# Binary cross-entropy on one core: compute pieces of 8192 columns in place of 2048, and larger chunks at both ends

## The chip, the cores and the metric

The kernel runs on one NeuronCore of one Trainium2 chip. The metric is the device time of one execution in microseconds (us), as the median of several executions.

## The reference

Two 8192 x 8192 fp32 arrays come in, one goes out. The target holds only zeros and ones.

```python
def reference(pred, target):
    eps = 1e-7
    pred = np.clip(pred, eps, 1 - eps)
    return -(target * np.log(pred) + (1 - target) * np.log(1 - pred))
```

Since the target is 0 or 1, the kernel computes -ln|target - 1 + clip(pred)|. The target is cast to bf16 while it is loaded.

## The kernel before

The 524288 columns (per partition) are cut into chunks that are loaded and stored whole, in a ring of 32768 columns, a buffer whose places are used again in turn. Two chunks of 16384 fit in it; each half is called a slot below. A chunk is computed in pieces of `SUB` = 2048 columns.

```python
RING = 32768
SUB = 2048
LAG = 1

def chunk_widths(total):
    head = [4096, 4096, 8192]
    tail = [8192, 4096, 2048, 1024, 1024]
    big = 16384
    ...                                            # 30 chunks of 16384 between them

def front(c, w):
    p, t = ring_p[:, c : c + w], ring_t[:, c : c + w]
    nc.vector.tensor_scalar(out=p, in0=p, ...)     # L88, clamp
    nc.vector.scalar_tensor_tensor(out=p, in0=t, scalar=1.0, in1=p, ...)   # L91, t - 1 + p
    nc.scalar.activation(out=p, in_=p, func=Act.Abs)                       # L94
    nc.scalar.activation(out=p, in_=p, func=Act.Ln)                        # L95

def back(c, w):
    nc.vector.tensor_scalar(out=p, in0=p, scalar1=-1.0, ...)               # L99, negate
...
def finish_one():
    nonlocal stored
    k, c, w, last = waiting.pop(0)
    back(c, w)
    if last:
        store(k)                # on the GpSimd queue
        stored = k + 1
        load_what_fits()        # target (cast), then prediction, GpSimd queue

for k, c, w, last in pieces:
    front(c, w)
    waiting.append((k, c, w, last))
    if len(waiting) > LAG:
        finish_one()
    if last and cols[k] + widths[k] <= total - RING // 2:
        while waiting:          # a chunk is finished before the next one begins
            finish_one()
```

## Time and profile before

| | before |
|---|---|
| time | 1873.39 us, median of 3 (1873.09 to 1873.55) |
| span of the profiled execution | 1873.0 us |
| instructions | 1564 (VectorE 772, ScalarE 516) |
| VectorE / ScalarE busy | 63% / 52% |
| HBM traffic | 805 MB, 430 GB/s over the span |
| one big chunk, landing to landing | 58.22 us |

The last row comes from the timeline: the first clamp of the first big chunk starts at 81.60 us, that of the last at 1769.93, with 29 chunks between them.

In the lines of the profile DVE is VectorE, ACT is ScalarE, POOL is GpSimd and SP is SyncE; a transfer is issued by an engine and lands when its data has arrived. These are lines of the page of the kernel before: busy time per engine (share of the span, number of instructions), the DMA row of the 40 slices (9 is 90% or more), and the DMA queues (packets, MB, share of the 16 engines' span).

```profile
span 1873.0 us, 1564 instructions
...
DVE 1178.3 (63%) x772; ACT 976.3 (52%) x516; POOL 64.2 (3%) x117
...
DMA  9999999999999999999999999999999999999997
...
q14 instruction: 11, 0.09, 0.0%
HBM read 536.87 MB, written 268.44 MB: 430 GB/s over the span
...
```

The reader is to see that DMA is full in 39 slices of 40 while neither compute engine is. Queue q14, which the profile labels instruction, is read here as the fetching of the instructions themselves.

These are groups of the same kernel with different shapes kept apart: count, then busy us and the mean ns of one, then idle time before them.

```profile
...
L91 DVE SCALAR_TENSOR_TENSOR ring_p<-ring_t,ring_p 128x2048 f32<-128x2048 bf16 x255 | 584.6, 2292 | 9.9 <-DMA ring_t<-in_target_dram 1.2
...
L88 DVE TENSOR_SCALAR ring_p<-ring_p 128x2048 f32<-128x2048 f32 x255 | 311.6, 1222 | 552.3 <-DMA ring_p<-in_pred_dram 552.3
...
L91 DVE SCALAR_TENSOR_TENSOR ring_p<-ring_t,ring_p 128x1024 f32<-128x1024 bf16 x2 | 2.5, 1226 | 0.1
...
```

An operation on 2048 columns takes nearly twice as long as on 1024 (2292 against 1226 ns), so the fixed part is only 2 x 1226 - 2292 = 160 ns.

Now the timeline of the kernel before, near the end: start, duration, engine, line, operation; in brackets the idle time before it and what ended it.

```profile
...
1731.55 0.53 POOL L80 DMA_DIRECT2D ring_p<-in_pred_dram  x1 [35.86 <-DMA out_dram<-ring_p]
...
1752.57 0.54 POOL L84 DMA_DIRECT2D out_dram<-ring_p  x1 [20.49 <-DVE ring_p L99]
...
1769.93 1.23 DVE L88 TENSOR_SCALAR ring_p<-ring_p 128x2048 f32<-128x2048 f32 x1 [17.66 <-DMA ring_p<-in_pred_dram]
...
1789.51 0.53 POOL L80 DMA_DIRECT2D ring_p<-in_pred_dram  x1 [35.88 <-DMA out_dram<-ring_p]
...
1808.89 1.48 POOL L80 DMA_DIRECT2D ring_p<-in_pred_dram  x1 [9.17 <-DMA ring_p<-in_pred_dram]
1809.02 1.23 DVE L99 TENSOR_SCALAR ring_p<-ring_p 128x2048 f32<-128x2048 f32 x1 [2.78 <-ACT ring_p L95]
...
1850.94 0.53 POOL L84 DMA_DIRECT2D out_dram<-ring_p  x1 [1.77 <-DVE ring_p L99]
```

This is how the rotation is read. A prediction load issued at 1731.55 lets a clamp start at 1769.93. The store of the other slot is issued at 1752.57, while that load is under way, and lands at 1789.51, when the waiting prediction load goes out. Each transfer waits for those issued before it. Compute of the chunk takes from 1769.93 to the end of the last negate at 1809.02 + 1.23, 40.3 us. The issue at 1808.89 took 1.48 us instead of 0.54: it ended with the negate beside it.

Finally two rows of who waited for whom (us in total, times, longest), of the kernel before.

```profile
...
POOL ring_p L80 <- DMA out_dram<-ring_p: 1087.8, 30, 37.1
...
DVE ring_p L88 <- DMA ring_p<-in_pred_dram: 552.3, 32, 18.5
...
```

GpSimd waits for stores to land in 30 chunks, and VectorE's clamp for loads, about 18 us a chunk. VectorE has time to spare.

### The profile page before, as it was taken

The numbers are of one execution on the slowest core, as the hardware profiler recorded it, in microseconds if no ns is written. First come the engines' busy times: TensorE is split into PE (matmuls) and PEld (weight loads), VectorE is DVE, ScalarE is ACT, GpSimd is POOL, SyncE is SP. The second block draws the span as 40 slices with busy tenths as digits, with TensorE's granted clock in tenths as the row PEclk, the third lists the DMA queues.
The fourth block names the chain that finished last, engine by engine and source line by source line (L and its number), as shares of the span: only waits on it lengthen the run. The fifth ranks groups of instructions, "written<-read, shape, count | busy, mean of one in ns | idle before, by whom it ended". The sixth has DMA issues, their size and how long they took to land.

```text
span 1873.0 us, 1564 instructions
## 1 busy us (share of the span) xinstructions
DVE 1178.3 (63%) x772; ACT 976.3 (52%) x516; POOL 64.2 (3%) x117
## 2 busy tenths in 40 slices
DVE  4557755577555775557755567655676556765594
ACT  3446544465444664446644466444564445654474
POOL 1000000000000000000000000000000000000010
DMA  9999999999999999999999999999999999999997
GB/s 302 359 347 346 347 392 385 341 336 358 383 386 350 337 351 377 393 352 339 353 366 392 363 337 353 357 393 373 337 348 350 393 385 336 340 357 384 393 319 323
DMA packets 16427, 671.19 MB, mean 358 GB/s; under 512 B 1824, under 2 KB 1824, under 8 KB 2720
## 3 DMA queue, kind: packets, MB, share of 16 engines
q0 software_dynamic: 16272, 669.00, 99.4%
q1 hardware_dynamic: 144, 2.10, 0.3%
q14 instruction: 11, 0.09, 0.0%
HBM read 536.87 MB, written 268.44 MB: 430 GB/s over the span
## 4 chain that ended last, share of the span: by engine, by line
DMA 36%; issue 27%; DVE 27%; ACT 7%; POOL 1%; another core or an unknown queue 1%; POOLq 0%; PEldq 0%
DMA ring_p<-in_pred_dram 32%; DVE ring_p L91 13%; DVE ring_p L99 7%; DVE ring_p L88 7%; DMA out_dram<-ring_p 4%; ACT ring_p L94 3%; ACT ring_p L95 3%; POOL out_dram L84 1%; POOL ring_t L75 0%; POOL ring_p L80 0%; POOLq L175 0%; POOLq L84 0%; PEldq L175 0%
## 5 line engine op out<-in xcount | busy, mean ns | idle before, releaser
L94 ACT ACTIVATE ring_p<-ring_p 128x2048 f32<-128x2048 f32 (+1 forms) x257 | 488.9, 1902 | 864.8 <-DVE ring_p L91 864.8
L88 DVE TENSOR_SCALAR ring_p<-ring_p 128x2048 f32<-128x2048 f32 (+1 forms) x257 | 313.0, 1218 | 552.3 <-DMA ring_p<-in_pred_dram 552.3
L91 DVE SCALAR_TENSOR_TENSOR ring_p<-ring_t,ring_p 128x2048 f32<-128x2048 bf16 (+1 forms) x257 | 587.0, 2284 | 10.0 <-DMA ring_t<-in_target_dram 1.2
L95 ACT ACTIVATE ring_p<-ring_p 128x2048 f32<-128x2048 f32 (+1 forms) x257 | 489.2, 1903 | 8.1
L99 DVE TENSOR_SCALAR ring_p<-ring_p 128x2048 f32<-128x2048 f32 (+1 forms) x257 | 313.0, 1218 | 109.3 <-ACT ring_p L95 109.3
L80 POOL DMA_DIRECT2D ring_p<-in_pred_dram x37 | 21.3, 576 | 1097.0 <-DMA out_dram<-ring_p 1087.8
L84 POOL DMA_DIRECT2D out_dram<-ring_p x38 | 21.7, 571 | 684.8 <-DVE ring_p L99 681.1
L75 POOL DMA_DIRECT2D ring_t<-in_target_dram x38 | 21.5, 567 | 5.3 <-DMA ring_t<-in_target_dram 4.4
L127 ACT ACT_TABLE_LOAD x1 | 1.3, 1283 | 0.7 <-PEq L164 0.7
L126 DVE MEMSET warm<- 1x8 f32 x1 | 0.1, 65 | 0.8 <-PEq L164 0.8
L127 ACT ACTIVATE warm<-warm 1x8 f32<-1x8 f32 x1 | 0.2, 208 | 0.0
L164 POOL MEMSET const-float32-0.0<- 128x1 f32 x1 | 0.1, 99 | 0.2 <-issue 0.2
L164 POOL MEMSET const-bfloat16-1.0<- 128x1 bf16 x1 | 0.1, 102 | 0.0
L164 POOL MEMSET const-float32-1.0<- 128x1 f32 x1 | 0.1, 100 | 0.0
L164 POOL MEMSET const-uint8-127<- 128x1 uint8 x1 | 0.1, 99 | 0.0
## 6 DMA issues: line engine op xcount, KB each, us to landing
ring_t<-in_target_dram POOLq DMA_DIRECT2D x30, 4096.0 KB, 55.8
ring_p<-in_pred_dram POOLq DMA_DIRECT2D x2, 4096.0 KB, 29.0
out_dram<-ring_p POOLq DMA_DIRECT2D x2, 4096.0 KB, 30.6
out_dram<-ring_p POOLq DMA_DIRECT2D x3, 2048.0 KB, 54.1
ring_p<-in_pred_dram POOLq DMA_DIRECT2D x2, 2048.0 KB, 24.2
ring_t<-in_target_dram POOLq DMA_DIRECT2D x2, 2048.0 KB, 37.8
ring_t<-in_target_dram POOLq DMA_DIRECT2D x3, 1024.0 KB, 16.2
ring_p<-in_pred_dram SPq DMA_DIRECT2D x1, 2048.0 KB, 10.2
```

What stands on the lines that cost most here:

```text
L75: nc.gpsimd.dma_start(out=ring_t[:, c : c + w], in_=dram(target_f, cols[k], w))
L80: queue.dma_start(out=ring_p[:, c : c + w], in_=dram(pred_f, cols[k], w))
L84: nc.gpsimd.dma_start(out=dram(out_f, cols[k], w), in_=ring_p[:, c : c + w])
L88: nc.vector.tensor_scalar(out=p, in0=p, scalar1=EPS, scalar2=1 - EPS, op0=Alu.max, op1=Alu.min)
L91: nc.vector.scalar_tensor_tensor(out=p, in0=t, scalar=1.0, in1=p, op0=Alu.subtract, op1=Alu.add)
L94: nc.scalar.activation(out=p, in_=p, func=Act.Abs)
L95: nc.scalar.activation(out=p, in_=p, func=Act.Ln)
L99: nc.vector.tensor_scalar(out=p, in0=p, scalar1=-1.0, scalar2=None, op0=Alu.mult)
L126: nc.vector.memset(warm, 1.0)
L127: nc.scalar.activation(out=warm, in_=warm, func=Act.Ln)
L164: nc = _bacc.Bacc("TRN2", target_bir_lowering=False, num_devices=1)
```

## The change

The intent is to do the compute with a quarter of the instructions: a chunk of 16384 columns becomes two pieces of 8192. Head and tail are loaded in chunks of 8192, and the last two chunks are stored piece by piece, so that the end still drains in small steps.

```diff
-SUB = 2048
-LAG = 1
-def chunk_widths(total):
-    head = [4096, 4096, 8192]
-    tail = [8192, 4096, 2048, 1024, 1024]
-    big = 16384
+BIG = 16384
+def plan(total):
+    head = [(8192, [4096, 4096]), (8192, [8192])]
+    tail = [(8192, [4096, 4096]), (8192, [4096, 2048, 1024, 1024])]
+    n = (total - sum(w for w, _ in head + tail)) // BIG
+    chunks = head + [(BIG, [BIG // 2] * 2)] * n + tail
...
+    def store(k, off, w):
+        nc.gpsimd.dma_start(
+            out=dram(out_f, k)[:, off : off + w], in_=span(ring_p, cols[k] + off, w)
+        )
...
+    def finish_one():
+        nonlocal stored
+        k, off, w = waiting.pop(0)
+        back(cols[k] + off, w)
+        if k >= tail:
+            store(k, off, w)
+        elif off + w == widths[k]:
+            store(k, 0, widths[k])
+        else:
+            return
+        stored = cols[k] + off + w
+        load_what_fits()
```

The operations of `front` and `back`, the ring and the queues stay as they were. In the changed kernel the clamp is L85, the subtract-add L88, Abs and Ln L91 and L92, the negate L96, the store L79, the prediction load L76.

More of the change, by code (lines that the diff above doesn't have):

```diff
@@ L12 @@
 RING = 32768
-SUB = 2048
-LAG = 1
-def chunk_widths(total):
-    head = [4096, 4096, 8192]
-    tail = [8192, 4096, 2048, 1024, 1024]
-    big = 16384
-    n = (total - sum(head) - sum(tail)) // big
-    widths = head + [big] * n + tail
-    assert sum(widths) == total
-    return widths
+BIG = 16384
[4 more added lines that the diff above has]
+    chunks = head + [(BIG, [BIG // 2] * 2)] * n + tail
+    assert sum(w for w, _ in chunks) == total
+    return chunks, len(chunks) - len(tail)
 @with_exitstack
@@ L55 @@
     total = R * C // P
-    def dram(flat, col, w):
-        return flat[col * P : (col + w) * P].rearrange("(p w) -> p w", p=P)
     pool = ctx.enter_context(tc.tile_pool(name="rings", bufs=1))
@@ L63, with dram, span, load @@
     warm = pool.tile([1, 8], fp32, name="warm", tag="warm")
-    widths = chunk_widths(total)
-    cols = [sum(widths[:k]) for k in range(len(widths))]
-    def at(k):
-        c = cols[k] % RING
-        assert c + widths[k] <= RING
-        return c
-    def load_t(k):
-        c, w = at(k), widths[k]
-        nc.gpsimd.dma_start(out=ring_t[:, c : c + w], in_=dram(target_f, cols[k], w))
-    def load_p(k):
-        c, w = at(k), widths[k]
-        queue = nc.sync if k == 0 else nc.gpsimd
-        queue.dma_start(out=ring_p[:, c : c + w], in_=dram(pred_f, cols[k], w))
-    def store(k):
-        c, w = at(k), widths[k]
-        nc.gpsimd.dma_start(out=dram(out_f, cols[k], w), in_=ring_p[:, c : c + w])
-    def front(c, w):
-        p, t = ring_p[:, c : c + w], ring_t[:, c : c + w]
+    chunks, tail = plan(total)
+    widths = [w for w, _ in chunks]
+    cols = [sum(widths[:k]) for k in range(len(chunks))]
+    def dram(flat, k):
+        part = flat[cols[k] * P : (cols[k] + widths[k]) * P]
+        return part.rearrange("(p w) -> p w", p=P)
+    def span(ring, col, w):
+        c = col % RING
+        assert c + w <= RING
+        return ring[:, c : c + w]
+    def load(k):
+        queue = nc.sync if k == 0 else nc.gpsimd
+        nc.gpsimd.dma_start(out=span(ring_t, cols[k], widths[k]), in_=dram(target_f, k))
+        queue.dma_start(out=span(ring_p, cols[k], widths[k]), in_=dram(pred_f, k))
+    def store(k, off, w):
+        nc.gpsimd.dma_start(
+            out=dram(out_f, k)[:, off : off + w], in_=span(ring_p, cols[k] + off, w)
+        )
+    def front(col, w):
+        p, t = span(ring_p, col, w), span(ring_t, col, w)
         nc.vector.tensor_scalar(
@@ L95, in front, with back @@
         nc.scalar.activation(out=p, in_=p, func=Act.Ln)
-    def back(c, w):
-        p = ring_p[:, c : c + w]
-        nc.vector.tensor_scalar(
-            out=p, in0=p, scalar1=-1.0, scalar2=None, op0=Alu.mult
-        )
-    pieces = []
-    for k, w in enumerate(widths):
-        n = max(1, w // SUB)
-        for i in range(n):
-            pieces.append((k, at(k) + i * (w // n), w // n, i == n - 1))
-    stored = 0
-    loaded = 0
+    def back(col, w):
+        p = span(ring_p, col, w)
+        nc.vector.tensor_scalar(out=p, in0=p, scalar1=-1.0, scalar2=None, op0=Alu.mult)
+    stored = loaded = 0
     def load_what_fits():
@@ L116, in load_what_fits @@
         while (
-            loaded < len(widths)
-            and cols[loaded] + widths[loaded] <= (cols + [total])[stored] + RING
-        ):
-            load_t(loaded)
-            load_p(loaded)
+            loaded < len(chunks) and cols[loaded] + widths[loaded] <= stored + RING
+        ):
+            load(loaded)
             loaded += 1
+    waiting = []
+    def finish_one():
[10 more added lines that the diff above has]
+        load_what_fits()
     with tc.manual_schedule():
@@ L127 @@
         nc.scalar.activation(out=warm, in_=warm, func=Act.Ln)
-        waiting = []
-        def finish_one():
-            nonlocal stored
-            k, c, w, last = waiting.pop(0)
-            back(c, w)
-            if last:
-                store(k)
-                stored = k + 1
-                load_what_fits()
-        for k, c, w, last in pieces:
-            front(c, w)
-            waiting.append((k, c, w, last))
-            if len(waiting) > LAG:
+        for k, (_, pieces) in enumerate(chunks):
+            off = 0
+            for w in pieces:
+                front(cols[k] + off, w)
+                waiting.append((k, off, w))
+                off += w
+                if len(waiting) > 1:
+                    finish_one()
+            while waiting and k < tail:
                 finish_one()
-            if last and cols[k] + widths[k] <= total - RING // 2:
-                while waiting:
-                    finish_one()
         while waiting:
```

## The prediction

> **What bounds the kernel now.** The DMA engines. In the page's 40 slices DMA stands at 9 tenths in 39. The stretches view gives a DMA share of 1.00 in every 116.5 us period, and near 1.00 from 4 to 1860 us. HBM traffic is 430 GB/s over the span. The Trainium skill ("DMA: Bandwidth & Descriptors", Specifications) gives 435 GB/s as the fabric ceiling; this trace agrees: two 16384-column chunks (50.3 MB) take 116.5 us, 432 GB/s. VectorE is 63% busy, ScalarE 52%.
>
> Transfers behave like one first-in-first-out list, about 19.4 us for one chunk's target load, prediction load or store: a prediction load lands 38.4 us after issue (a target load is ahead of it), a store 37, a target load 55.8. The rotation is store k, target k+2, prediction k+2, store k+1. A bubble opens only if store k+1 is issued after prediction k+2 lands, so a chunk's compute may take about 58 us less the start of a transfer, some 56 us. In the timeline it takes 40.3 us (1769.9 to 1810.3).
>
> **What the change does.** 257 pieces become 69: VectorE 772 to about 208 instructions, ScalarE 516 to about 140. By the groups kept apart by shape, 1024/2048 columns take 0.69/1.22 us (clamp, negate), 1.23/2.29 (subtract-add), 1.05/1.91 (Abs, Ln): a fixed part of only 0.15 to 0.2 us. I estimate 4.4, 8.7 and 7.0 us at 8192 columns; VectorE sheds about 54 us of busy time, ScalarE about 75, none on the critical path.
>
> What grows is the fill of the pipeline in each chunk: two fronts 26 us, Ln of the second piece ends at 41, the last negate at 45.7. Compute per chunk goes from 40.3 to about 46 us; about 10 us of slack remain.
>
> Issue blocking: the Trainium skill ("SBUF — State Buffer", the "DVE blocks DMA" trap) says that GpSimd cannot write descriptors during a two-port VectorE instruction. The trace agrees: issues beside a clamp or negate took 0.96 to 1.48 us instead of 0.54, ending 0.1 us after it. At 8192 columns a block may last 4.4 us. In the steady state stores are issued with VectorE idle, and the prediction load falls into the second subtract-add with a target load still queued: no bubble.
>
> Head: the first 32768 columns are issued at once in both kernels and keep the DMA busy to 81.6 us; the first two stores come at about 47 and 80 us, in time. Tail: the loads end near 1828 us; the last big store is issued near 1818, the piece stores at 1832 to 1857, each before its turn. The list ends as before. The 4.4 and 9.2 us issue waits before the last small loads, which cost nothing, disappear. DMA operations fall from 114 to 106, bytes unchanged.
>
> **Prediction: 1873 us, range 1867 to 1880.** Faster by over 2%: 0.01; within 2%: 0.97; slower: 0.02.
>
> **What would show it.** DMA share 1.00 in periods of 116.5 us; VectorE near 1125 us busy, ScalarE near 901; the clamp's wait for the prediction load falls from about 18 to about 12 us per chunk; stores land about 31 us after issue instead of 37; the last store issued near 1857.
>
> **What would make it wrong.** Compute above 56 us per chunk (large pieces slower than linear), costing 30 times the excess; issues blocked while the list is empty, most likely at 80 us and 1815 to 1857, a few us each; transfers that share rather than queue, making the end ragged. A gain is bounded by idle DMA time at both ends, about 15 us, under 1%.

## The result, and the profile after

The changed kernel took 1870.31 us (median of 4, 1869.79 to 1871.81), the kernel before 1873.24 us in the same rounds (1872.40 to 1873.55). The ratio is 0.9986 with a 95% interval of 0.9969 to 1.0004: the same at 2%. Ratios here are the mean time of one kernel's fast runs over that of the other's of the same rounds, so not quite the ratio of the medians quoted.

The same lines of the page, of the changed kernel:

```profile
span 1868.4 us, 607 instructions
...
DVE 1121.7 (60%) x208; ACT 899.7 (48%) x140; POOL 63.5 (3%) x109
...
DMA  9999999999999999999999999999999999999998
...
q14 instruction: 4, 0.03, 0.0%
HBM read 536.87 MB, written 268.44 MB: 431 GB/s over the span
...
```

Instructions fell from 1564 to 607 and VectorE's busy time by 57 us, ScalarE's by 77. The DMA row is as full as before, and the rate over the span is 431 instead of 430 GB/s. Of the 4.6 us by which the profiled spans differ, the steady state has 3.2: a big chunk takes 58.11 us from landing to landing instead of 58.22 (81.37 to 1766.49 us, 29 chunks). The profiled execution of the kernel before was 1.4 us above that kernel's median (1874.81 against 1873.39 us), so the profiles differ by more than the times do.

The groups of the changed kernel, shapes kept apart:

```profile
...
L88 DVE SCALAR_TENSOR_TENSOR ring_p<-ring_t,ring_p 128x8192 f32<-128x8192 bf16 x61 | 530.2, 8692 | 2.1
L92 ACT ACTIVATE ring_p<-ring_p 128x8192 f32<-128x8192 f32 x61 | 428.8, 7029 | 1.9
...
L85 DVE TENSOR_SCALAR ring_p<-ring_p 128x8192 f32<-128x8192 f32 x61 | 269.8, 4423 | 365.0 <-DMA ring_p<-in_pred_dram 365.0
...
```

The estimates of the prediction from 1024 and 2048 columns (8.7, 7.0 and 4.4 us) hold at 8192.

The timeline of the changed kernel, at the head and near the end:

```profile
...
43.88 4.42 DVE L85 TENSOR_SCALAR ring_p<-ring_p 128x8192 f32<-128x8192 f32 x1
44.27 4.16 POOL L79 DMA_DIRECT2D out_dram<-ring_p  x1 [40.20 <-DVE ring_p L96]
...
1754.54 0.54 POOL L79 DMA_DIRECT2D out_dram<-ring_p  x1 [25.89 <-DVE ring_p L96]
...
1766.49 4.43 DVE L85 TENSOR_SCALAR ring_p<-ring_p 128x8192 f32<-128x8192 f32 x1 [12.24 <-DMA ring_p<-in_pred_dram]
...
1786.09 0.54 POOL L76 DMA_DIRECT2D ring_p<-in_pred_dram  x1 [30.47 <-DMA out_dram<-ring_p]
...
1807.78 4.43 DVE L96 TENSOR_SCALAR ring_p<-ring_p 128x8192 f32<-128x8192 f32 x1 [9.55 <-ACT ring_p L92]
1812.12 2.29 DVE L85 TENSOR_SCALAR ring_p<-ring_p 128x4096 f32<-128x4096 f32 x1
1812.51 2.03 POOL L79 DMA_DIRECT2D out_dram<-ring_p  x1 [24.83 <-DVE ring_p L96]
...
1852.85 0.53 POOL L79 DMA_DIRECT2D out_dram<-ring_p  x1 [1.77 <-DVE ring_p L96]
```

Four things are to be seen. The store is now issued at 1754.54, only 12 us before the clamp of the next chunk starts at 1766.49; it lands at 1786.09, after 31.5 us. The chunk's compute lasts from 1766.49 to the end of the negate at 1807.78 + 4.43, 45.7 us instead of 40.3. Two store issues, at 44.27 and 1812.51, took 4.16 and 2.03 us and ended about 0.1 us after the clamp beside them. And the last store is issued at 1852.85, later than before (1850.94), yet the kernel ends earlier.

The two rows of waits, of the changed kernel:

```profile
...
POOL ring_p L76 <- DMA out_dram<-ring_p: 912.8, 30, 31.5
...
DVE ring_p L85 <- DMA ring_p<-in_pred_dram: 384.4, 31, 19.4
...
```

The clamp now waits 12 us a chunk for its load instead of 18, because compute takes longer; the load comes at the same time. No issue of a load waits for another load any more, as it did for 4.44 and 9.17 us in the tail of the kernel before.

### The profile page after: what moved, and what is told of

Read it like the earlier page. It is cut to its first block, busy times and chain, and to the rows that moved or that the text cites. A ratio compares the mean times of both kernels' runs of the same rounds, so it can differ in the third digit from the quotient of the medians.

```text
span 1868.4 us, 607 instructions
## 1 busy us (share of the span) xinstructions
DVE 1121.7 (60%) x208; ACT 899.7 (48%) x140; POOL 63.5 (3%) x109
## 4 chain that ended last, share of the span: by engine, by line
DMA 33%; issue 25%; ACT 24%; DVE 15%; POOL 1%; POOLq 0%; DVEq 0%; PEldq 0%
DMA ring_p<-in_pred_dram 31%; ACT ring_p L92 12%; ACT ring_p L91 12%; DVE ring_p L88 8%; DVE ring_p L85 4%; DVE ring_p L96 4%; DMA out_dram<-ring_p 1%; DMA ring_t<-in_target_dram 1%; POOL out_dram L79 1%; POOL ring_t L75 0%; POOLq L165 0%; POOLq L79 0%; DVEq L88 0%; PEldq L165 0%; POOLq L76 0%
## 5 line engine op out<-in xcount | busy, mean ns | idle before, releaser
L91 ACT ACTIVATE ring_p<-ring_p 128x8192 f32<-128x8192 f32 (+3 forms) x69 | 450.4, 6528 | 949.2 <-DVE ring_p L88 949.2
L88 DVE SCALAR_TENSOR_TENSOR ring_p<-ring_t,ring_p 128x8192 f32<-128x8192 bf16 (+3 forms) x69 | 557.1, 8074 | 2.5 <-DMA ring_t<-in_target_dram 0.2
L85 DVE TENSOR_SCALAR ring_p<-ring_p 128x8192 f32<-128x8192 f32 (+3 forms) x69 | 283.9, 4114 | 384.4 <-DMA ring_p<-in_pred_dram 384.4
L96 DVE TENSOR_SCALAR ring_p<-ring_p 128x8192 f32<-128x8192 f32 (+3 forms) x69 | 284.1, 4117 | 343.1 <-ACT ring_p L92 343.1
L92 ACT ACTIVATE ring_p<-ring_p 128x8192 f32<-128x8192 f32 (+3 forms) x69 | 450.9, 6535 | 2.2
L79 POOL DMA_DIRECT2D out_dram<-ring_p x38 | 27.4, 721 | 876.1 <-DVE ring_p L96 876.1
L76 POOL DMA_DIRECT2D ring_p<-in_pred_dram x33 | 17.6, 534 | 912.8 <-DMA out_dram<-ring_p 912.8
## 6 DMA issues: line engine op xcount, KB each, us to landing
ring_p<-in_pred_dram SPq DMA_DIRECT2D x1, 4096.0 KB, 19.5
```

The costliest lines, as they stand in the source:

```text
L76: queue.dma_start(out=span(ring_p, cols[k], widths[k]), in_=dram(pred_f, k))
L79: nc.gpsimd.dma_start(out=dram(out_f, k)[:, off : off + w], in_=span(ring_p, cols[k] + off, w))
L85: nc.vector.tensor_scalar(out=p, in0=p, scalar1=EPS, scalar2=1 - EPS, op0=Alu.max, op1=Alu.min)
L96: nc.vector.tensor_scalar(out=p, in0=p, scalar1=-1.0, scalar2=None, op0=Alu.mult)
```

## The experiments

Twelve kernels ran. All were correct, except e3, which is wrong on purpose. Times of "before" come from the same rounds. Each diff is against the changed kernel, but for e2, which is against the kernel before.

### k1_after_again: is the small difference real?

No edit.

> The changed kernel once more, five rounds. Theory F (the kernel is bound by its list of transfers, the 3 us are a real but small difference somewhere in the transfers): 1870 us, ratio 0.998 to 0.999 with an interval that leaves out 1. Theory N (the 3 us are the spread between executions): the ratio comes within 0.0005 of 1.

Measured: 1870.39 us (5 runs, 1869.69 to 1871.44) against 1872.93 us (9 runs, 1872.23 to 1874.58); ratio 0.9986, interval 0.9973 to 0.9998. The difference is small and clear of zero. Its size is about 2.5 us.

### e1_narrow_pieces and e2_wide_pieces_only: piece width or transfer plan?

```diff
@@ -18,6 +18,6 @@
 
-    head = [(8192, [4096, 4096]), (8192, [8192])]
+    head = [(8192, [2048] * 4), (8192, [2048] * 4)]
     tail = [(8192, [4096, 4096]), (8192, [4096, 2048, 1024, 1024])]
     n = (total - sum(w for w, _ in head + tail)) // BIG
-    chunks = head + [(BIG, [BIG // 2] * 2)] * n + tail
+    chunks = head + [(BIG, [2048] * 8)] * n + tail
     assert sum(w for w, _ in chunks) == total
```

> The changed kernel's transfers, head, tail and stores, but pieces of 2048 columns again in every chunk before the last two. Theory F with the gain in the piece width (steady state: each big chunk 0.11 us shorter in the trace of after): back to about 1873. Rival: the gain is in the transfer plan (8 fewer transfers, other tail): stays at 1870. Under either the first-in-first-out model says the time moves by less than 5 us, and the clamp's wait for the prediction load returns to about 18 us per chunk.

Measured: 1872.73 us (1872.38 to 1873.04), ratio to before 0.9998 (0.9984 to 1.0012).

```diff
@@ -105,3 +105,3 @@
     for k, w in enumerate(widths):
-        n = max(1, w // SUB)
+        n = 2 if w == 16384 else max(1, w // SUB)
         for i in range(n):
```

> The kernel before with nothing changed but two pieces of 8192 in each chunk of 16384; its own head, tail and 114 transfers stay. Gain in the piece width: about 1870. Gain in the transfer plan: stays at 1873. Wait of the clamp about 12 us per chunk in both cases.

Measured: 1870.80 us (1870.56 to 1871.26), ratio 0.9987 (0.9975 to 1.0000). The two together settle which half of the change counts. The new transfer plan alone gives nothing measurable, 1872.7; the wide pieces alone give the whole 2 us, 1870.8; the ranges of the two do not overlap. The clamp waited 556 us in e1 and 392 in e2 (totals of the wait view), 17 to 18 and about 12 us a chunk, without any effect on the time.

### e3_no_compute: where is the floor?

```diff
@@ -83,2 +83,3 @@
     def front(col, w):
+        return
         p, t = span(ring_p, col, w), span(ring_t, col, w)
@@ -94,2 +95,3 @@
     def back(col, w):
+        return
         p = span(ring_p, col, w)
```

> Wrong result on purpose: the changed kernel with front and back left out, so that each store waits for its load alone. If the transfers bound the kernel and compute is hidden completely: 1866 to 1871 us, the time of the changed kernel. If compute still costs something (gaps between transfers, or compute slowing the transfers): clearly below, by 10 us or more.

Measured: 1870.05 us (1868.91 to 1871.09); ratio to before 0.9983 (0.9970 to 0.9995). Its page:

```profile
span 1868.3 us, 158 instructions
...
DMA  9999999999999999999999999999999999999998
...
```

A kernel that only moves the data takes as long as the changed kernel. So the changed kernel hides its compute completely, within the spread of the runs, and the compute of the kernel before had cost no more than about 3 us.

### e4, e5 and e6: how much slack had the compute?

```diff
@@ -113,2 +113,5 @@
         back(cols[k] + off, w)
+        if widths[k] == BIG and off:
+            for _ in range(2):
+                back(cols[k] + off, w)
         if k >= tail:
```

> The changed kernel with the last negate of each of the 30 big chunks done three times (result stays right): 8.9 us more compute per chunk, about 54.6 us in all. Theory F with the slack of the prediction (compute may take some 56 us): 1869 to 1874 us, at the edge. Theory of a critical compute: 30 x 8.9 = 265 us more, about 2135.

Measured: 1888.57 us (2 runs), ratio 1.0082 (1.0062 to 1.0102): 18 us more than the changed kernel. Neither theory had this. A critical compute would have cost 265 us, so nearly all of it was still hidden; but the edge is not sharp. The timeline of e4:

```profile
...
1250.15 0.54 POOL L79 DMA_DIRECT2D out_dram<-ring_p  x1 [34.83 <-DVE ring_p L96]
...
1254.20 4.43 DVE L85 TENSOR_SCALAR ring_p<-ring_p 128x8192 f32<-128x8192 f32 x1 [4.34 <-DMA ring_p<-in_pred_dram]
...
1273.94 0.53 POOL L76 DMA_DIRECT2D ring_p<-in_pred_dram  x1 [22.72 <-DMA out_dram<-ring_p]
...
1312.57 4.43 DVE L85 TENSOR_SCALAR ring_p<-ring_p 128x8192 f32<-128x8192 f32 x1 [3.72 <-DMA ring_p<-in_pred_dram]
...
```

The store was issued 4 us before the clamp started, so before its turn; VectorE still had 4 us of wait. But the store landed 19.7 us after the clamp's start (19.6 in the changed kernel) and the prediction load 38.6 us after its issue (38.4). This chunk took 58.37 us. Over all 29 chunks the mean is 58.6 us instead of 58.1, because every second one took 58.8 to 59.9 us; its prediction load landed about 39.4 us after its issue. The 64 KB packets, which make up most of the traffic, took 2449 ns in the mean instead of 2423 (averaged from the packet records), with a median of 2418 ns in both: a few packets are slow, not all of them. Why these slow down when a store comes only 3 to 5 us ahead of its turn was not tested and stays open, and so does whether the slower packets are the cause of the loss or its mark.

```diff
@@ -113,2 +113,5 @@
         back(cols[k] + off, w)
+        if widths[k] == BIG and off:
+            for _ in range(4):
+                back(cols[k] + off, w)
         if k >= tail:
```

> The last negate of each big chunk done five times: 17.7 us more compute per chunk, about 63.4 us. Past the edge: a model with one first-in-first-out list gives 163 us more, 2030 us (1990 to 2070), with the list empty about 5.4 us in each of 30 chunks. If transfers share the engines instead of queueing, or the slack is much larger than 10 us: below 1930.

Measured: 2056.45 us (2 runs), at the upper half of the band. A chunk's compute is 63.6 us in its timeline (1235.77 to 1299.33). Thirty times 63.56 - 58.11 is 163.5 us, the model's number. The clamp's waits come to 42.2 us, of which 19.5 are the first load; the other 22.7 us are the rest of the difference of the spans, 2054.6 - 1868.4 = 186.2.

```diff
@@ -21,3 +21,3 @@
     n = (total - sum(w for w, _ in head + tail)) // BIG
-    chunks = head + [(BIG, [BIG // 2] * 2)] * n + tail
+    chunks = head + [(BIG, [BIG])] * n + tail
     assert sum(w for w, _ in chunks) == total
```

> The changed kernel with each big chunk in one piece of 16384, a further halving of the instructions. By linear pieces the chunk's compute is 8.7 + 17.2 + 2 x 13.8 + 8.7 = 62.4 us, past the edge: the model gives about 2000 us (1960 to 2040), although the engines' busy time falls again. If only the number of instructions counted: 1867 to 1870.

Measured: 2114.46 us (2 runs), far outside the band. Halving the instructions again made the kernel 13% slower than before. The compute of a chunk is 62.45 us (1203.56 to 1266.01 in its timeline), so 30 x 4.34 = 130 us were expected, and 113 us more came on top. The timeline of e6 shows where from:

```profile
...
1194.95 8.69 DVE L96 TENSOR_SCALAR ring_p<-ring_p 128x16384 f32<-128x16384 f32 x1 [27.81 <-ACT ring_p L92]
1203.56 8.69 DVE L85 TENSOR_SCALAR ring_p<-ring_p 128x16384 f32<-128x16384 f32 x1
1203.94 8.43 POOL L79 DMA_DIRECT2D out_dram<-ring_p  x1 [42.18 <-DVE ring_p L96]
...
1234.16 0.53 POOL L76 DMA_DIRECT2D ring_p<-in_pred_dram  x1 [21.26 <-DMA out_dram<-ring_p]
...
1273.76 8.69 DVE L85 TENSOR_SCALAR ring_p<-ring_p 128x16384 f32<-128x16384 f32 x1 [7.75 <-DMA ring_p<-in_pred_dram]
...
```

The negate of a chunk ends at 1203.64. The data of the next chunk has long landed, so its clamp starts at once, and the store, issued at 1203.94, is held for 8.43 us, to the end of that clamp. It lands at 1234.16, the prediction load goes out then, and at 1273.76 the clamp of the chunk after has waited 7.75 us for it. In sum over the kernel (the wait view of e6):

```profile
...
DVE ring_p L85 <- DMA ring_p<-in_pred_dram: 132.4, 16, 19.4
...
```

Less the first load, 19.4 us, this is 113.0 us, which closes the account: 130 + 113 = 243, against 2112.3 - 1868.4 = 243.9 of the spans. The 22.7 us of e5 have the same form: every second store there took 4.16 us to issue.

### e10_one_piece_sp_stores and e11_two_pieces_sp_stores: is the held issue the cause?

```diff
@@ -21,3 +21,3 @@
     n = (total - sum(w for w, _ in head + tail)) // BIG
-    chunks = head + [(BIG, [BIG // 2] * 2)] * n + tail
+    chunks = head + [(BIG, [BIG])] * n + tail
     assert sum(w for w, _ in chunks) == total
@@ -78,3 +78,3 @@
     def store(k, off, w):
-        nc.gpsimd.dma_start(
+        nc.sync.dma_start(
             out=dram(out_f, k)[:, off : off + w], in_=span(ring_p, cols[k] + off, w)
```

> One piece of 16384 per big chunk, as in e6, but stores issued from the sync engine's queue. In e6 every second store issue took 8.43 us beside the next clamp, and the clamp then waited 7.75 us for the prediction load of every second chunk, 113 us in all. If the block of GpSimd's descriptor writing did that: about 2000 us (1975 to 2025), 30 chunks of 62.4 us, and the clamp's wait falls under 20 us in total after the first. If the excess of e6 has another cause: 2080 or more.

Measured: 2015.46 us (2 runs), inside the band, 99 us below e6. The wait view of e10:

```profile
...
DVE ring_p L85 <- DMA ring_p<-in_pred_dram: 41.0, 2, 21.5
...
```

Of the 41.0 us, the longest wait, 21.5 us, is the first load; 19.5 remain, against 113 in e6. VectorE now runs chunk after chunk, 62.4 us apart. With the chain seen in e6's timeline, this supports that holding the store's issue beside the clamp was the cause of the excess in e6. One reservation: the edit also gives stores a list of their own.

```diff
@@ -78,3 +78,3 @@
     def store(k, off, w):
-        nc.gpsimd.dma_start(
+        nc.sync.dma_start(
             out=dram(out_f, k)[:, off : off + w], in_=span(ring_p, cols[k] + off, w)
```

> Control for e10 and a try at a better version: the changed kernel with only its stores moved to the sync engine's queue. The issues blocked in the changed kernel (4.16 us at the head, 2.03 twice in the tail) are off the critical path, so 1869 to 1872 us, no gain. If they cost something: 1862 to 1867. If two queues that share the engines are worse than one list: 1875 or more.

Measured: 1953.93 us (4 fast runs, 1952.81 to 1954.90), ratio 1.0431: the third case of the expectation, far beyond its number. The issues of e11 (size where it is known, and median us from issue to landing):

```profile
...
out_dram<-ring_p SPq DMA_DIRECT2D x30, 40.6
```

A store now takes 40.6 us to land, in place of 31.3 in the changed kernel (medians). The prediction load of the slot waits for that landing, and the clamp waits 479 us in total instead of 384. The Trainium skill ("DMA: Bandwidth & Descriptors", Issuing engines are not separate DMA queues) says that DMAs issued by different engines run on the same 16 engines and interleave. This trace agrees. These are the two queues (packets, MB, share of the 16 engines' span) from 1280 to 1300 us of e11, with a prediction load (q0) and a store (q1) in flight:

```profile
...
q0 software_dynamic: 64, 4.19, 48.4%
q1 hardware_dynamic: 64, 4.19, 48.4%
...
```

Each gets half, so the store no longer has its turn. The order changed too: a target load no longer stands behind the store in GpSimd's program, and goes out ahead of it (at 1209.60 us, the store at 1228.83). How the 84 us divide between the two was not tested. The same edit that saves 99 us in e6 costs 84 us here, so e11 was no better version, and it is no neutral control either. e10 therefore shows that the held issue is avoidable, and by how much the sum falls, but not the price of the second list within it.

### e7_last_chunk_whole: does the tail count?

```diff
@@ -19,3 +19,3 @@
     head = [(8192, [4096, 4096]), (8192, [8192])]
-    tail = [(8192, [4096, 4096]), (8192, [4096, 2048, 1024, 1024])]
+    tail = [(8192, [4096, 4096]), (8192, [8192])]
     n = (total - sum(w for w, _ in head + tail)) // BIG
```

> The changed kernel with the last chunk of 8192 computed and stored in one piece. If the piece stores of the tail matter as the prediction has it (each comes before its turn in the list): the last store is issued about 7 to 12 us later and the list runs empty before it, 1877 to 1883 us. If the tail is not on the critical path: 1870.

Measured: 1879.37 us (4 runs), ratio 1.0034 (1.0017 to 1.0051), as expected for a tail that counts. The stretches of the end, for e7 (busy us of VectorE, ScalarE, GpSimd, granted clock, DMA share, GB/s):

```profile
...
1850.00:1860.00 10.00, 3.69 (x1) 6.28 (x1) 0.00 (x0) 1.00 0.13 54
...
```

and for the changed kernel (k1):

```profile
...
1850.00:1860.00 10.00, 1.62 (x3) 2.11 (x2) 1.06 (x2) 1.00 0.97 412
...
```

With the last chunk in one piece, the list of transfers is nearly empty from 1850 to 1860 us (share 0.13); the last store is issued at 1861.03 instead of 1852.85. With piece stores the share is 0.97 there. Most bytes of the tail must be queued before their turn, and pieces do that. The edit makes both the compute and the store of the last chunk whole; the two were not separated.

### e8_30_tiny and e9_90_tiny: instruction count at constant width

The width of the pieces gave the 2.5 us, but width brings several things: fewer instructions, fewer fetches of instructions (q14: 11 packets before, 4 after, 11 in e1, 5 in e2, 1 in e3), longer clamps. These two runs add small instructions and next to no work.

```diff
@@ -58,2 +58,3 @@
     warm = pool.tile([1, 8], fp32, name="warm", tag="warm")
+    tiny = pool.tile([1, 8], fp32, name="tiny", tag="tiny")
 
@@ -112,2 +113,5 @@
         k, off, w = waiting.pop(0)
+        if widths[k] == BIG and off:
+            for _ in range(30):
+                nc.vector.memset(tiny, 1.0)
         back(cols[k] + off, w)
```

> The changed kernel with 30 memsets of 8 elements of one partition ahead of the last negate of each big chunk, where VectorE idles 9.5 us: 900 instructions more, as many as the change took away, and no other work. Theory I (the 2 to 3 us are instruction count: each further fetch of 8 KB of instructions, 309 ns in the trace, goes through a DMA engine that is already full; the kernel before shows 11 fetches in the steady state, the changed one 4): about 7 more fetches, 2.2 us, so about 1872.5. Rival (width of the pieces itself, or issue blocked by clamps): 1870.3.

Measured: 1875.42 us (5 runs, 1875.15 to 1876.23). That is 5.0 us above the changed kernel and above the kernel before too (ratio 1.0013, interval 1.0000 to 1.0026). The page of e8:

```profile
span 1873.5 us, 1507 instructions
...
q14 instruction: 11, 0.09, 0.0%
...
```

```diff
@@ -58,2 +58,3 @@
     warm = pool.tile([1, 8], fp32, name="warm", tag="warm")
+    tiny = pool.tile([1, 8], fp32, name="tiny", tag="tiny")
 
@@ -112,2 +113,5 @@
         k, off, w = waiting.pop(0)
+        if widths[k] == BIG and off:
+            for _ in range(90):
+                nc.vector.memset(tiny, 1.0)
         back(cols[k] + off, w)
```

> The same with 90 memsets a chunk, 2700 instructions more, still inside the 9.5 us in which VectorE idles. Theory I: about 21 more fetches x 309 ns = 6.5 us if all go through one DMA engine, so 1876 to 1877 (1870.7 if they are spread evenly over the 16). Rival: 1870.3.

Measured: 1887.96 us (5 runs, 1887.03 to 1888.77), 17.6 us above the changed kernel. The page of e9:

```profile
span 1887.0 us, 3307 instructions
...
q14 instruction: 25, 0.20, 0.0%
...
```

The rival, width itself, falls as the only reason: at constant width, small instructions that leave the chunk's compute within its slack lengthen a DMA-bound kernel. The fetches came as expected, 7 and 21 more. But the size is wrong: 5.0 and 17.6 us, where 309 ns for each fetch gives 2.2 and 6.5. In e9 the clamp still waits 11 to 12 us a chunk, so this is no lost slack; the steady state has it, 58.69 us a chunk.

The traces show where the time goes. These are the 16 chunks of each trace that begin after 800 us and are followed by another wait of the clamp, from clamp start to clamp start in us, sorted by whether a q14 packet starts in them:

| kernel | chunks without a fetch | chunks with a fetch |
|---|---|---|
| before | 11: 57.95 to 58.38 | 5: 58.64, 57.95, 58.63, 57.97, 58.61 |
| changed | 15: 57.94 to 58.02 | 1: 57.97 |
| e1 | 11: 57.92 to 57.99 | 5: 58.55, 57.97, 58.64, 57.96, 58.65 |
| e8 | 11: 57.94 to 57.97 | 5: 58.65, 58.49, 58.64, 58.63, 58.93 |
| e9 | 4: 58.00 to 58.21 | 12: 58.53 to 59.11 |

Thirty memsets in a chunk without a fetch cost nothing, ninety up to 0.2 us. In e8 a chunk with a fetch took 0.71 us more in the mean (58.67 against 57.96), and seven times that is an estimate of 5.0 us, the whole of what was measured. So theory I had the right carrier and less than half its price. Why a packet of 309 ns costs its chunk 0.5 to 1 us, and why two fetches of five cost nothing in the kernel before and in e1, stays open. Before 800 us chunks vary more in every kernel (58.3 us in the mean even in the changed one), and there the sorting shows less.

The series of this document, by instructions:

| kernel | instructions | q14 packets | us |
|---|---|---|---|
| e3, no compute | 158 | 1 | 1870.05 |
| k1, the changed kernel | 607 | 4 | 1870.39 |
| e2, wide pieces only | 663 | 5 | 1870.80 |
| e1, narrow pieces | 1534 | 11 | 1872.73 |
| before | 1564 | 11 | 1872.93 |
| e8, 30 memsets a chunk | 1507 | 11 | 1875.42 |
| e9, 90 memsets a chunk | 3307 | 25 | 1887.96 |

The runs were made on three chips (k1 to e3, e4 to e7, e8 to e11), but the kernel before agrees on them within 0.2 us (1872.93, 1873.15, 1873.06). e8 and e1 have nearly the same number of instructions and the same number of packets, and differ by 2.7 us. So the number alone does not fix the time; in the table by chunk, fetches without cost occur in e1 and not in e8. From 607 to 158 instructions nothing measurable is gained.

## Why the prediction was right

- **The bound.** DMA share 1.00 and 58.2 us a chunk were taken as a floor that the change does not move. e3 shows the floor directly: 1870.05 us without any compute. The forecast of 1873 us, 1867 to 1880, held at 1870.3.
- **What moved off the critical path.** VectorE was forecast at 1125 us and came to 1121.7, ScalarE 901 and 899.7; compute per chunk about 46 us and 45.7; the clamp's wait about 12 us and 12.2; the store's landing about 31 us after issue and 31.5. All these are large changes in the profile, and none of them is in the time.
- **The tail.** "each before its turn" held: the last store was forecast near 1857 and issued at 1852.85, and the DMA stayed full to about 1858. e7 shows what it costs when this fails, 9 us.
- **Held issues.** "At 8192 columns a block may last 4.4 us": 4.16 us at the head, 2.03 beside the 4096-column clamps of the tail, both harmless. The Trainium skill ("SBUF — State Buffer", A bandwidth-pool intuition that's wrong) says a blocked issue ends at the end of the VectorE instruction plus about 115 ns. This trace agrees: 43.88 + 4.42 = 48.30 us for the clamp, 44.27 + 4.16 = 48.43 for the issue.
- **The step that was off: "none on the critical path"**, said of the busy time shed. It holds for the busy time, but the instructions that went with it had a small price: the transfers ran at 58.11 instead of 58.22 us a chunk. The prediction looked for a gain only in "idle DMA time at both ends", and in the profiles most of it came in the steady state. e1 and e2 put the 2.5 us on the narrow pieces; e8 and e9 show that extra small instructions alone lengthen the kernel, in the chunks with a fetch. In the kernel before, the three long chunks with a fetch after 800 us make up 2.0 us of the 3.2 us of the steady state. That the 957 instructions taken away gave the rest in this way is argued and not shown, and each trace is one execution.
- **The term that was mis-sized: slack.** "About 10 us of slack remain" and "costing 30 times the excess". With 8.9 us more the list did not run empty, and yet 18 us were lost (e4). Beyond the edge the cost is the excess plus the wait for loads behind held store issues, 23 us in e5 and 113 in e6, which the prediction named only as "a few us each" in the head and the tail.

## What to carry to other kernels

When a kernel moves its bytes at the rate of a copy with no compute at all, a large cut in compute instructions is worth only what those instructions disturb in the transfers; run the copy once to know the floor before tuning. Wider pieces cost pipeline fill in every chunk: keep the chunk's compute below the time of the other transfers in the rotation by a margin (a clamp that waited 12 us a chunk was enough here, 3 to 5 us was not), and check that a store is issued while no long VectorE instruction follows at once, or a held issue enters the chain. At the end of such a kernel, computing and storing in pieces, so that stores are queued before their turn, was worth more (9 us) than fewer instructions (2.5 us).

## What the Trainium skill lacked or had wrong

- "HBM Reference" (Specifications (TRN2)) says a core streaming alone measures about 425 GB/s, limited by its DMA engines. This trace agrees and is slightly above: 431 GB/s over the whole span, with stores and a cast in the mix, counted by the bytes on the HBM side (on the SBUF side the target has half its bytes, and the page of the profile has 359 GB/s). "SBUF — State Buffer" (A bandwidth-pool intuition that's wrong) puts HBM to a core at about 358 GB/s, half of a stack's, and from that calls HBM nearly always the bottleneck. For a core that runs alone, as here, that figure is too low by 73 GB/s.
- "SBUF — State Buffer" (the "DVE blocks DMA" trap) advises to issue from the scalar or sync queue. Doing so with the stores saved 99 us in e6's schedule and cost 84 us in the changed kernel (e11). The page lacks that stores on a second queue can lose their turn to the loads of the first (40.6 us to landing instead of 31.3).
- No page that was found gives a price for the number of instructions beside a full set of DMA engines. "DMA: Bandwidth & Descriptors" (Queues, rings and completion order) only lists a runtime-internal queue row, 14. Here that queue is labelled instruction, and 900 memsets of 65 ns each cost 5.0 us (e8), 2700 cost 17.6 us (e9). "Runtime: NRT & Kernel Launch" (Instruction fetch mechanics) does describe the fetching: in blocks of 16 KiB, 256 instructions, at a cost mostly hidden. Here a packet has 8 KB, 2700 memsets brought 21 of them, about 129 each, and in e8 a chunk with one took 0.71 us more.
- No page that was found describes the soft edge of e4: 18 us lost while stores were still issued 3 to 5 us before the next clamp could start.
